# Sums over partitions by transposes, the second half's keys in other PSUM rings, and one 1/rms by way of DRAM, in a hybrid decoder layer

## The chip, the cores and the metric

The kernel runs on one core of a Trainium2 chip. The metric is the device time of one execution in microseconds; lower is better. The core has a matrix engine (TensorE, PE in the profile), VectorE (DVE), ScalarE (ACT), GpSimd (POOL) and SyncE (SP), whose queue issues most DMAs. All matrix results land in PSUM, eight banks of 128 x 512 f32 values.

## The reference

One decoder layer over 2048 tokens of 1024 channels: a norm, one projection into an HGRN2 head group and a sliding-window attention group, an output projection, a gated MLP with a causal convolution, and a final norm. Cut to what matters here:

```python
def rmsnorm(x, w, eps=EPS):
    xf = x.astype(jnp.float32)
    inv = lax.rsqrt(jnp.mean(xf * xf, axis=-1, keepdims=True) + eps)
    return (xf * inv * w.astype(jnp.float32)).astype(x.dtype)

u = rmsnorm(h, norm_mix_w[l])
proj = u @ w_in[l]
...
h = h + mix @ w_out[l]
v = rmsnorm(h, norm_ffn_w[l])
gate = causal_depthwise_conv(v @ w_gate[l], conv_w[l], conv_b[l])
h = h + (jax.nn.silu(gate) * (v @ w_up[l])) @ w_down[l]
...
return rmsnorm(h, final_norm_w)
```

Each of the three norms needs, for each token, the sum of the squares over 1024 channels, and 1/rms from it.

## The kernel before

Activations are kept transposed: channels on the 128 partitions, tokens along the row. The sequence is worked in two halves of 1024 tokens (`hf`, `HALF`), and a half in two token halves `lo` and `hi` of 512. Every matrix product is made of three products of split operands (`hi` and `lo` parts, in fp32r), each a matmul over 512 tokens.

A half goes through these stages: keys and values (`first_unit`, twice: the list `kv`), the heads in an order written out by hand (`ORDER`, with `hgrn` and `attend`), the output projection (`out_proj`), gate and up products (`gate_up`) and the down product (`down`). Gate, up and down use a scheme with seven products instead of eight (`PRODUCTS`: P1, P5, P6, P3, P7, P2, P4, in six pieces each). `down` of the first half also loads and squares the x of the second half, and at its end issues the second half's `kv` and the first `f` product (L1008 to L1010), with the remaining norm work hooked in between their matmuls by `then`. In the last half the product P4 is made token block by token block instead, in `last_rows` (L1013), with tokens on the partitions, and its results leave through the output `rows`.

The program is written out by a tile framework. It places each instruction on its engine in an order that comes from its own model of times, gives tiles their slots, and adds the semaphore waits. On the chip each engine then runs its own queue in that fixed order.

PSUM has three rings: `mm` with four banks, `hg` and `at` with two each; `aux` (L72) names the last two. `unit` (L189) takes one bank for each token half, from `mm`, or from `hg` and `at` for `kind="aux"`. In `down` the products P1, P6, P7 and P4 sit in `mm` (tile `pdx`), P5, P3 and P2 in `hg` and `at` (tile `pdy`).

The norm's 1/rms goes in three steps.

- `Stats.add` (L232) adds squares over the channel blocks into `acc`, 128 partitions by 512 or 1024 tokens.
- `Stats.inverse` (L239) sums over the partitions: for each chunk of 128 tokens one matmul, with the chunk as the stationary operand and a column of ones as the moving one, gives a column with one token per partition (tile `pst`, L245). `rsqrt` (L156) then makes 1/rms on DVE, 13 small instructions on 128 x 4 or 128 x 8 values (L159 to L169).
- `Stats.spread` (L250) brings 1/rms back to all partitions: for each chunk one transpose of the broadcast column (tile `pinv`, L258), and for each 512 tokens a copy by ACT out of PSUM into `acc` (L261).

In `down`, `s1` holds the sums of the final norm for `lo`, `s2` those for `hi`. `finish` (L1081) multiplies the eight blocks of h by 1/rms on DVE (L1084) and sends them out on SP's queue (L1085). For `s2` it runs while P4 is still being made or, in the last half, inside `last_rows`; for `s1` of the first half it runs during the second half's `kv`. `last_rows` makes its own sums of `s1` (L1034) for the partial mean of each token row (`base`), and for each block of 128 tokens takes 1/rms on DVE, scales the rows out of PSUM, and later transposes 1/rms (L1073) for the channels that stay transposed.

Of the kernel before, what the change touches and what calls it, by code (L numbers as in the profile page):

```python
# [8 lines left out]
F32 = mybir.dt.float32  # L9
# [4 lines left out]
ALU = mybir.AluOpType  # L14
AX = mybir.AxisListType
PSUM = bass.MemoryType.PSUM

P = 128
D = 1024
# [7 lines left out]
ATT_J = 4  # L27
# [3 lines left out]
EPS = 1e-6  # L31
# [18 lines left out]
def hymba_layer(ctx: ExitStack, tc: tile.TileContext, a: dict, out: bass.AP, rows_out: bass.AP):  # L50
    nc = tc.nc
# [11 lines left out]
    dp = pool("dram", space=bass.MemoryType.DRAM)  # L63
# [5 lines left out]
    def ps(kind, name):  # L69
        return spaces[kind].tile([P, 512], F32, tag=kind, name=name)  # L70

    aux = ("hg", "at")  # L72

    def halves():
# [5 lines left out]
    ones = cp.tile([P, P], F32, name="ones")  # L80
    nc.vector.memset(ones, 1.0)
    ident = cp.tile([P, P], F32, name="ident")
# [5 lines left out]
                            base=0, pattern=[[-1, P]], channel_multiplier=1)  # L88
# [64 lines left out]

    made = []

    def rsqrt(ss, n, scale, keep=None):  # L156

        ms = sp.tile([P, n], F32, tag=f"ms{n}", name="ms")
        nc.vector.tensor_scalar(ms, ss, scale, EPS, op0=ALU.mult, op1=ALU.add)  # L159
        y = sp.tile([P, n], F32, tag=f"y{n}{keep}", name="y")  # L160
        yi = y.bitcast(I32)
        nc.vector.tensor_scalar(yi, ms.bitcast(I32), 1, None, op0=ALU.logical_shift_right)
        nc.vector.tensor_scalar(yi, yi, -1.0, float(0x5F3759DF), op0=ALU.mult, op1=ALU.add)
        nc.vector.tensor_scalar(ms, ms, -0.5, None, op0=ALU.mult)
        t = sp.tile([P, n], F32, tag=f"t{n}", name="t")
        for _ in range(3):
            nc.vector.tensor_tensor(t, y, y, op=ALU.mult)
            nc.vector.tensor_tensor(t, t, ms, op=ALU.mult)
            made.append(nc.vector.scalar_tensor_tensor(y, t, 1.5, y, op0=ALU.add, op1=ALU.mult))  # L169
        return y  # L170
# [51 lines left out]
    class Stats:  # L222
# [16 lines left out]
        def inverse(self, keep):  # L239

            n = self.acc.shape[-1]
            nt = n // P
            st = ps("hg", "pst")
            for c in range(nt):
                nc.tensor.matmul(st[:, c:c + 1], self.acc[:, c * P:(c + 1) * P], ones[:, 0:1],  # L245
                                 start=True, stop=True)
            self.rs = rsqrt(st[:, 0:nt], nt, 1.0 / D, keep)
            return made[-1]

        def spread(self, bank=None):  # L250

            n = self.acc.shape[-1]
            w = min(n, 512)
            for b in range(n // w):
                pb = ps(aux[b % 2 if bank is None else bank], "pinv")[:, 0:w]
                for c in range(w // P):
                    i = b * w // P + c
                    nc.tensor.transpose(pb[:, c * P:(c + 1) * P], self.rs[:, i:i + 1].to_broadcast([P, P]), ident)  # L258
                if bank is not None:
                    return pb  # L260
                nc.scalar.copy(self.acc[:, b * w:(b + 1) * w], pb)  # L261

    def inv_tile():
        return xp.tile([P, HALF], F32, tag="inv", name="invb", bufs=1)
# [44 lines left out]
            st.add(x)  # L309
        return st  # L310

    def first_unit(X, W, i, then={}):
        return unit(tuple(W[i]) if W else a["w_att"][ATT_J + i], X, "kv", then=then)

    def blocks(t, turn=False):

# [541 lines left out]
    def down(hf, kept, acts, p):  # L858
# [54 lines left out]
        hh = []  # L913
# [37 lines left out]
        for k, (name, _, _, j) in enumerate(todo):  # L951
            if k + 2 < len(todo):
                ready[k + 2] = prep_piece(k + 2)
            if j == 0:
                if name == "P1":
                    bx = o = [ps("mm", "pdx") for _ in range(4)]
                elif name in ("P5", "P2"):
                    by = o = [ps(aux[d % 2], "pdy") for d in range(4)]
                else:
                    o = by if name == "P3" else bx  # L960
                if name == "P3":
                    acc = inv_tile() if final else wp.tile([P, HALF], F32, tag="raw", name="sums", bufs=RAW)
                    s1, s2 = [Stats(acc[:, bs], lambda: p.tile([P, 512], F32, tag="ut", name="fsq", bufs=UT))
                              for bs in (lo, hi)]
                if name == "P2" and not final:
                    stage = iter(("xh2", "xl2") * (KT // 2))
                    loading = load(hf + 1, X, lambda: p.tile([P, HALF], F32, tag=next(stage), name="x", bufs=6))
            if not final and k >= end - 3:
                xs = next(loading, xs)
            if final and k == end:  # L970
                break
            if k == end + 1:
                s2.inverse("o2")
            elif k == end + 3:
                s2.spread()
                finish(hf, hh, s2, hi, nc.sync)
            for d in range(4):
                product(k, o[d], d)
            if j + 1 < NP:
                continue  # L980
            for d in range(4):
                h1, h2 = hh[d], hh[d + 4]
                if name in ("P1", "P2"):
                    add(h1[:, lo], o[d])
                elif name in ("P6", "P3"):
                    add(h1[:, hi], o[d])
                elif name in ("P5", "P7"):
                    add(h2[:, hi], o[d])
                    if final and name == "P7":
                        add(h2[:, lo], o[d])  # L990
                else:
                    add(h2[:, lo], o[d])
                if name == "P3":
                    done(s2, d, hi)
                elif name == "P7":
                    done(s2, d + 4, hi)
                elif name == "P2":
                    done(s1, d, lo)
                elif name == "P4":
                    done(s1, d + 4, lo)  # L1000
        if final:
            for k in range(end + 3, len(todo)):
                ready[k] = prep_piece(k)
            last_rows(hf, hh, s1, fw, ready, range(end, len(todo)), p,
                      {(0, 1): lambda: s2.inverse("o2"),
                       (0, 3): lambda: (s2.spread(), finish(hf, hh, s2, hi, nc.sync))})
            return None
        kv = [first_unit(X, None, 0, {3: lambda: s1.inverse("o"), 7: lambda: xs.inverse("x")})]  # L1008
        kv.append(first_unit(X, None, 1, {2: lambda: (s1.spread(), finish(hf, hh, s1, lo, nc.sync)), 4: xs.spread}))
        f0 = unit(a["w_f"][0], X, "f", kind="aux")  # L1010
        return X, kv, xs.acc, xs.rs, f0

    def last_rows(hf, hh, st, fw, ready, pieces, p, then):  # L1013
# [9 lines left out]
        for tb in range(4):  # L1023
# [5 lines left out]
            for n, k in enumerate(pieces):  # L1029
                then.pop((tb, n), lambda: None)()  # L1030
                if (tb, n) == (0, 4):
                    sb = ps("hg", "pst")
                    for c in range(4):
                        nc.tensor.matmul(sb[:, c:c + 1], st.acc[:, c * P:(c + 1) * P], ones[:, 0:1],  # L1034
                                         start=True, stop=True)
                    base = sp.tile([P, 4], F32, tag="base", name="base")
                    nc.vector.tensor_scalar(base, sb[:, 0:4], 1.0 / D, EPS, op0=ALU.mult, op1=ALU.add)
                    half = sp.tile([P, 4], F32, tag="half", name="half")
                    nc.vector.tensor_scalar(half, base, -0.5, None, op0=ALU.mult)
                if (tb, n) == (0, 5):  # L1040
                    o1 = ps("at", "rows1")
                    for d in range(4):
                        nc.tensor.transpose(o1[:, d * P:(d + 1) * P], hh[d][:, 3 * P:4 * P], ident)
                    y1 = ut("y1")
                    nc.scalar.copy(y1, o1)
                (ah, al), (wh, wl) = ready[k]
                for i in range(wh.shape[1]):
                    l = k == pieces[-1] and i + 1 == wh.shape[1]
                    nc.tensor.matmul(o, ah[:, i, ts], wh[:, i], start=False, stop=False, skip_group_check=True)
                    nc.tensor.matmul(o, ah[:, i, ts], wl[:, i], start=False, stop=False, skip_group_check=True)  # L1050
                    nc.tensor.matmul(o, al[:, i, ts], wh[:, i], start=False, stop=l, skip_group_check=True)
# [29 lines left out]
    def finish(hf, hh, st, bs, eng, inv=None):  # L1081
        for d in range(KT):
            t = hh[d][:, bs]
            nc.vector.tensor_tensor(t, t, st.acc if inv is None else inv, op=ALU.mult)  # L1084
            eng.dma_start(out[d, :, hf * HALF + bs.start:hf * HALF + bs.stop], t)  # L1085

    X, W = [], []
# [105 lines left out]
```

## Time and profile before

| what | us |
|---|---|
| median of 3 runs | 2155.03 |
| lowest and highest | 2154.21, 2155.93 |
| profiled execution, device time | 2156.06 |
| profiled execution, span from first to last instruction | 2154.3 |
| mean granted TensorE clock in it | 0.999 |

The profile is one execution. Its span starts with the first instruction and ends with the last; the device time has a little more around it. In a timeline row stand the start in us from the span's beginning, the duration in us, the engine, the source line, the operation, the output tile and the input tiles, the shapes and the count of merged instructions; a bracket tells how long the engine was idle before and what released it. PEld is the loading of TensorE's stationary operand. Of a matmul's inputs the moving one is named first. Busy time of matmuls overlaps, so what a matmul costs is read from the starts of the ones around it.

### The profile page before, as it was taken

Reading aid. Unit: us, or ns where it says so; the run is one execution under the profiler, and the core shown is the slowest. Engines: PE = TensorE matmul, PEld = TensorE weight load, DVE = VectorE, ACT = ScalarE, POOL = GpSimd, SP = SyncE. Lnnn points to the kernel's source line nnn. Section 1 sums busy time; section 2 is a strip of 40 time slices with the busy share of each in tenths; the row PEclk is TensorE's granted clock in tenths of the full one; section 3 lists DMA queues with packets and bytes.
Section 4 is the critical chain, followed back from the end, with each engine's and each line's share of the span. In section 5 each row is a group of like instructions: output and inputs, shape, how many; then the busy total and the mean of one; then the engine's idle time right before and its main releaser. Section 6 shows DMA issues by size and latency. Waiting matters only on the chain.

```text
span 2154.3 us, 29259 instructions
## 1 busy us (share of the span) xinstructions
PE 2136.6 (99%) x11319; PEld 1797.8 (83%) x11319; DVE 1622.7 (75%) x2431; ACT 1021.1 (47%) x1818; POOL 19.5 (1%) x45
## 2 busy tenths in 40 slices
PE   8999999999999999999999999999999999999998
PEld 7988988888888888888889889888888888888887
DVE  6576767788887878785865767677888788787865
ACT  5445553564444445335634446525544444443453
POOL 2000000000000000000000000000000000000000
PEclk9999999999999999999999999999999999999999
DMA  4111112423232334964641101124233323259743
GB/s 158 40 30 40 31 30 79 137 70 126 83 127 84 113 107 158 382 231 161 201 137 33 37 30 31 40 74 157 70 105 101 119 84 127 88 190 395 236 147 132
DMA packets 91148, 254.42 MB, mean 118 GB/s; under 512 B 11137, under 2 KB 13953, under 8 KB 91009
## 3 DMA queue, kind: packets, MB, share of 16 engines
q1 hardware_dynamic: 90576, 252.29, 35.0%
q8 instruction: 89, 1.46, 0.3%
q14 instruction: 51, 0.41, 0.1%
q10 hardware_dynamic: 432, 0.27, 0.0%
HBM read 195.37 MB, written 57.15 MB: 117 GB/s over the span
## 4 chain that ended last, share of the span: by engine, by line
PE 94%; DVE 3%; ACT 1%; DMA 1%; issue 1%; SPq 0%; DVEq 0%; ACTq 0%
PE X L753 7%; PE X L755 7%; PE X L754 7%; PE pop L204 7%; PE f L204 4%; PE q L204 4%; PE hq L204 4%; PE Y L754 4%; PE Y L753 4%; PE Y L755 4%; PE g L204 3%; PE pdy L940 3%; PE pdx L940 3%; PE pdx L941 3%; PE pdx L942 3%; PE pdy L941 3%
## 5 line engine op out<-in xcount | busy, mean ns | idle before, releaser
L628 ACT CAST whi<-raw 128x1024 fp32r<-128x1024 f32 x88 | 92.5, 1051 | 101.7 <-PE X L754 68.3
L824 DVE SCALAR_TENSOR_TENSOR y<-ga,cw,y 128x1024 f32<-128x1024 f32 x88 | 112.2, 1277 | 37.7 <-ACT y L822 37.7
L753 PE MATMUL X<-T,whi 128*128 128x512 f32 x352 | 136.9, 389 | 0.0
L754 PE MATMUL X<-T,whi 128*128 128x512 f32 x352 | 136.9, 389 | 0.0
L755 PE MATMUL X<-T,wlo 128*128 128x512 f32 x352 | 136.9, 389 | 0.0
L629 DVE TENSOR_TENSOR wlo<-raw,whi 128x1024 fp32r<-128x1024 f32 x88 | 107.1, 1217 | 5.6 <-ACT whi L628 5.6
L185 ACT CAST whi<-raw 128x1024 fp32r<-128x1024 f32 x58 | 60.5, 1048 | 103.1 <-issue 20.6
L759 ACT COPY u<-X 128x512 f32<-128x512 f32 x88 | 51.7, 588 | 99.6 <-PE X L755 99.4
L629 DVE TENSOR_TENSOR xld<-raw,xhd 128x1024 fp32r<-128x1024 f32 x72 | 80.8, 1130 | 10.4 <-ACT xhd L628 10.3
L628 ACT CAST xhd<-raw 128x1024 fp32r<-128x1024 f32 x72 | 69.4, 977 | 35.9 <-DMA raw<-act0B 10.7
L204 PE MATMUL pop<-XL,whi 128*128 128x512 f32 x256 | 84.2, 392 | 0.9 <-DVE XL L216 0.9
L204 PE MATMUL pop<-XH,wlo 128*128 128x512 f32 x256 | 83.3, 391 | 0.8 <-DVE wlo L186 0.8
L204 PE MATMUL pop<-XH,whi 128*128 128x512 f32 x256 | 83.2, 396 | 0.8 <-ACT XH L215 0.5
L186 DVE TENSOR_TENSOR wlo<-raw,whi 128x1024 fp32r<-128x1024 f32 x58 | 70.3, 1216 | 11.0 <-ACT whi L185 11.0
L753 PEld LDWEIGHTS X<-T,whi 128*128 128x128 f32 x352 | 66.1, 188 | 13.7
L755 PEld LDWEIGHTS X<-T,wlo 128*128 128x128 f32 x352 | 66.1, 188 | 13.7
L754 PEld LDWEIGHTS X<-T,whi 128*128 128x128 f32 x352 | 66.1, 188 | 13.7
L759 ACT COPY s<-X 128x512 f32<-128x512 f32 x44 | 25.9, 588 | 106.4 <-PE X L755 106.4
L621 PE MATMUL pvv<-whi,XL 128*128 128x256 f32 x256 | 73.0, 286 | 0.0
L620 PE MATMUL pvv<-whi,XH 128*128 128x256 f32 x256 | 72.9, 286 | 0.0
L622 PE MATMUL pvv<-wlo,XH 128*128 128x256 f32 x256 | 72.1, 285 | 0.0
L753 PE MATMUL X<-T,Sh 128*128 128x512 f32 x176 | 68.7, 390 | 0.0
(390 smaller groups left out, 6440.2 us busy)
## 6 DMA issues: line engine op xcount, KB each, us to landing
wr<-in_w_down SPq DMA_DIRECT2D x90, 512.0 KB, 5.7
raw<-in_w_gate SPq DMA_DIRECT2D x44, 512.0 KB, 3.6
raw<-in_w_up SPq DMA_DIRECT2D x44, 512.0 KB, 3.6
raw<-act0T SPq DMA_DIRECT2D x20, 512.0 KB, 5.4
raw<-act1T SPq DMA_DIRECT2D x20, 512.0 KB, 5.0
act0B<-y SPq DMA_DIRECT2D x33, 256.0 KB, 2.6
act1B<-y SPq DMA_DIRECT2D x33, 256.0 KB, 2.3
raw<-in_w_out SPq DMA_DIRECT2D x16, 512.0 KB, 3.7
```

Of the source, the lines that this page charges most:

```text
L204: nc.tensor.matmul(o[b], w, x[:, bs], start=f, stop=l)
L620: nc.tensor.matmul(o[:, 0:256], xh[:, t], hi[:, c], start=kt == 0, stop=False)
L621: nc.tensor.matmul(o[:, 0:256], xl[:, t], hi[:, c], start=False, stop=False)
L628: nc.scalar.copy(h, src)
L629: return (eng or nc.vector).tensor_tensor(l, src, h.bitcast(F32), op=ALU.subtract)
L753: nc.tensor.matmul(o, wh[:, ws], xh, start=i == 0 and not more, stop=False, skip_group_check=more)
L754: nc.tensor.matmul(o, wh[:, ws], xl, start=False, stop=False, skip_group_check=more)
L755: nc.tensor.matmul(o, wl[:, ws], xh, start=False, stop=i == 3, skip_group_check=more)
L759: nc.scalar.copy(t, o)
L824: nc.vector.scalar_tensor_tensor(y, g[:, w:w + HALF], C.cw[:, ft, w:w + 1], y, op0=ALU.mult, op1=ALU.add)
L940: nc.tensor.matmul(o, wh[:, i, c], ah[:, i, cols], start=f, stop=False, skip_group_check=more)
L941: nc.tensor.matmul(o, wh[:, i, c], al[:, i, cols], start=False, stop=False, skip_group_check=more)
```

## The change

There are three edits.

1. Sums over partitions: a new helper `sums` transposes up to four chunks of `acc` into one bank and lets DVE add each transposed chunk along the row. `rsqrt` calls it where `keep` is given, which is in every `Stats.inverse`; eight chunks take one bank of `hg` and one of `at`. `last_rows` calls it for `base`. The heads' own norm (`rsqrt(ss, TT, 1.0 / P)`) is as before.
2. Keys of the second half: the first of the two `kv` units takes its banks from `hg` and `at`, and the `f` product behind them from `mm`. In the first half `kv` and `f` are as before.
3. 1/rms of `s2` in both halves: `spread_far` writes the 128 x 4 values as one row of 512 into DRAM and loads that row to all 128 partitions, both by DMAs of GpSimd's queue, in place of the transposes and the copy of `spread`.

```diff
+    def sums(dst, acc):
+
+        n = acc.shape[-1] // P
+        for c0 in range(0, n, 4):
+            k = min(4, n - c0)
+            st = ps(aux[c0 // 4 % 2], "pst")
+            for c in range(k):
+                nc.tensor.transpose(st[:, c * P:(c + 1) * P], acc[:, (c0 + c) * P:(c0 + c + 1) * P], ident)
+            nc.vector.tensor_reduce(dst[:, c0:c0 + k], st[:, 0:k * P].rearrange("p (c t) -> p c t", c=k),
+                                    axis=AX.X, op=ALU.add)
+
     def rsqrt(ss, n, scale, keep=None):
 
         ms = sp.tile([P, n], F32, tag=f"ms{n}", name="ms")
+        if keep:
+            sums(ms, ss)
+            ss = ms
         nc.vector.tensor_scalar(ms, ss, scale, EPS, op0=ALU.mult, op1=ALU.add)
...
-            st = ps("hg", "pst")
-            for c in range(nt):
-                nc.tensor.matmul(st[:, c:c + 1], self.acc[:, c * P:(c + 1) * P], ones[:, 0:1],
-                                 start=True, stop=True)
-            self.rs = rsqrt(st[:, 0:nt], nt, 1.0 / D, keep)
+            self.rs = rsqrt(self.acc, nt, 1.0 / D, keep)
             return made[-1]
...
+    def spread_far(st, dst):
+
+        row = dp.tile([1, 512], F32, name="row")
+        nc.gpsimd.dma_start(row.rearrange("o (c p) -> (o p) c", p=P), st.rs)
+        nc.gpsimd.dma_start(dst, row.to_broadcast([P, 512]))
...
-    def first_unit(X, W, i, then={}):
-        return unit(tuple(W[i]) if W else a["w_att"][ATT_J + i], X, "kv", then=then)
+    def first_unit(X, W, i, then={}, kind="mm"):
+        return unit(tuple(W[i]) if W else a["w_att"][ATT_J + i], X, "kv", kind=kind, then=then)
...
             elif k == end + 3:
-                s2.spread()
+                spread_far(s2, s2.acc)
                 finish(hf, hh, s2, hi, nc.sync)
...
-                       (0, 3): lambda: (s2.spread(), finish(hf, hh, s2, hi, nc.sync))})
+                       (0, 3): lambda: (spread_far(s2, s2.acc), finish(hf, hh, s2, hi, nc.sync))})
...
-        kv = [first_unit(X, None, 0, {3: lambda: s1.inverse("o"), 7: lambda: xs.inverse("x")})]
+        kv = [first_unit(X, None, 0, {3: lambda: s1.inverse("o"), 7: lambda: xs.inverse("x")}, "aux")]
         kv.append(first_unit(X, None, 1, {2: lambda: (s1.spread(), finish(hf, hh, s1, lo, nc.sync)), 4: xs.spread}))
-        f0 = unit(a["w_f"][0], X, "f", kind="aux")
+        f0 = unit(a["w_f"][0], X, "f")
...
-                    sb = ps("hg", "pst")
-                    for c in range(4):
-                        nc.tensor.matmul(sb[:, c:c + 1], st.acc[:, c * P:(c + 1) * P], ones[:, 0:1],
-                                         start=True, stop=True)
                     base = sp.tile([P, 4], F32, tag="base", name="base")
-                    nc.vector.tensor_scalar(base, sb[:, 0:4], 1.0 / D, EPS, op0=ALU.mult, op1=ALU.add)
+                    sums(base, st.acc)
+                    nc.vector.tensor_scalar(base, base, 1.0 / D, EPS, op0=ALU.mult, op1=ALU.add)
```

## The prediction

> **What bounds the kernel now.** I read the totals and the chain of the page first, then the engine waits, and then TensorE's (PE's) timeline at each place that the diff touches.
>
> ```profile
> span 2154.3 us, 29259 instructions
> PE 2136.6 (99%) x11319; PEld 1797.8 (83%) x11319; DVE 1622.7 (75%) x2431; ACT 1021.1 (47%) x1818; POOL 19.5 (1%) x45
> ...
> PE 94%; DVE 3%; ACT 1%; DMA 1%; issue 1%; SPq 0%; DVEq 0%; ACTq 0%
> ...
> PE kv L204 <- ACT XH L218: 5.9, 1, 5.9
> ```
>
> The first two lines are the span and the busy times, the third is the chain that ended last by engine, the last is the longest wait of PE (total, times, longest). PE is nearly the whole chain, and what it waits longest for is one wait of 5.9 us, for the first input. So an edit is worth what it takes out of PE's instruction stream, or puts between two of its matmuls. Work of DVE (VectorE), ACT and the queues counts only when PE, or the last rows behind PE, waits for it.
>
> **The sums over partitions.** Before, four 128x1 matmuls make the sums of 512 tokens; the trace has each of them as two passes. After, four transposes do it, and DVE adds up along the row.
>
> ```profile
> L245 PE MATMUL pst<-ones,invb 128*128 128x1 f32 x72 | 8.4, 242 | 0.0
> L258 PE MATMUL pinv<-ident,y 128*128 128x128 f32 x44 | 5.9, 272 | 0.0
> ...
> L245 PE MATMUL pst<-ones,sums 128*128 128x1 f32 x16 | 1.9, 239 | 0.0
> L1034 PE MATMUL pst<-ones,invb 128*128 128x1 f32 x8 | 0.9, 240 | 0.0
> ```
>
> 72 + 16 + 8 = 96 passes are 48 chunks of 128 tokens, or 12 groups of four. The mean of one matmul (242, 272 ns) misleads, because matmuls overlap; the starts tell the cost:
>
> ```profile
> 1047.91 0.39 PE L942 MATMUL pdx<-xh2d,lod 128*128 128x512 f32 x1
> 1048.14 0.95 PE L245 MATMUL pst<-ones,sums 128*128 128x1 f32 x8
> ...
> 1049.74 0.40 PE L940 MATMUL pdx<-xh2d,gad 128*128 128x512 f32 x1
> ...
> 1078.16 0.39 PE L204 MATMUL kv<-XL,whi 128*128 128x512 f32 x1
> 1078.38 0.60 PE L258 MATMUL pinv<-ident,y 128*128 128x128 f32 x4
> ...
> 1079.52 0.39 PE L204 MATMUL kv<-XH,whi 128*128 128x512 f32 x1
> ```
>
> Full-width matmuls start 0.227 us apart (1047.91 to 1048.14). In both extracts the last row is the fourth full-width matmul after the first, so 0.91 us would lie between them without the group. There are 1.83 us with the sums and 1.36 with four transposes: **0.92 us against 0.45**. The transposes here have the shape of the new ones (128 columns of the identity, a 128x128 stationary block in f32). Twelve groups save 12 x 0.47 = **5.6 us**.
>
> DVE gets 12 reductions of 128x512 out of PSUM; the trace has none.
>
> ```profile
> L428 DVE TENSOR_TENSOR po<-ppt,ownT 128x512 f32<-128x512 f32 x32 | 21.8, 683 | 1.9 <-PE ppt L425 1.9
> L401 DVE TENSOR_REDUCE m<-sc 128x8 f32<-128x1024 f32 x16 | 19.4, 1214 | 0.2
> ```
>
> A 512-column read of PSUM takes 0.68 us, a reduction of twice the elements 1.21, hence 0.61: between 0.6 and 0.7 us each, some 8 us on an engine that is idle for a quarter of the span. I cost it at nothing, because the chain from the sums to the transposes of 1/rms ends early on DVE:
>
> ```profile
> 463.24 0.16 DVE L169 SCALAR_TENSOR_TENSOR y<-t,y 128x8 f32<-128x8 f32 x1
> ...
> 467.43 1.01 PEld L258 LDWEIGHTS pinv<-ident,y 128*128 128x128 f32 x8
> ...
> 1091.40 0.17 DVE L169 SCALAR_TENSOR_TENSOR y<-t,y 128x8 f32<-128x8 f32 x1
> ...
> 1096.82 1.03 PE L258 MATMUL pinv<-ident,y 128*128 128x128 f32 x8
> ```
>
> From the last step of 1/rms to its transposes there are 4.0 us in the gated MLP and 5.3 at the change of halves; one or two reductions take at most 1.4 of that. Were this cover gone, each of the seven places with sums would cost PE up to 1.4 us. The sums of eight chunks also take a bank of the second auxiliary ring, `at`; it is free again after the reduction, before the products `Y` and `Z` and the transposes at 467 us ask for the rings.
>
> **1/rms of the last norm's second token half by DRAM.** On PE, `s2.spread()` goes twice, each one group of four transposes: 2 x 0.45 = **0.9 us**. Two ACT copies go too, worth nothing on an engine busy 47%. Added are two DMAs on the queue of POOL (GpSimd), the second waiting for the first: 512 single numbers to a row in DRAM, then the row to all partitions. Behind them in POOL's queue stand only memsets of `ST` for the heads to come (POOL is busy 19.5 us in all). Eight DVE multiplications wait for the second DMA, and behind these, in DVE's order, stand the sums of the first token half and of the next half's x; on SP eight output DMAs wait, with weight loads behind them.
>
> ```profile
> 1074.85 0.15 DVE L169 SCALAR_TENSOR_TENSOR y<-t,y 128x4 f32<-128x4 f32 x1
> ...
> 1080.55 4.91 DVE L1084 TENSOR_TENSOR h<-h,sums 128x512 f32<-128x512 f32 x8 [0.27 <-ACT sums L261]
> ...
> 2123.04 0.16 DVE L169 SCALAR_TENSOR_TENSOR y<-t,y 128x4 f32<-128x4 f32 x1
> 2127.59 4.91 DVE L1084 TENSOR_TENSOR h<-h,invb 128x512 f32<-128x512 f32 x8 [4.39 <-ACT invb L261]
> ...
> 2138.82 0.38 PE L1073 MATMUL pinv<-ident,yr 128*128 128x128 f32 x2
> ...
> fw<-in_final_norm_row SPq DMA_DIRECT2D x1, 256.0 KB, 3.1
> rows<-y ACTq DMA_DIRECT2D x2, 128.0 KB, 2.2
> nmw<-in_norm_mix_w ACTq DMA_DIRECT2D x1, 4.0 KB, 3.2
> battn<-in_b_attn SPq DMA_DIRECT2D x1, 3.0 KB, 8.6
> ```
>
> Before, the multiplications start 5.5 and 4.4 us after 1/rms is done. No DMA of POOL is in the trace; the last column of the DMA rows is the time from issue to landing. A broadcast of a row like the second DMA took 3.1 us, a small load of 32-byte pieces 3.2; the lower bound is two of the fastest, 4.4, the upper two of the slowest, 17.2. I take 3.2 + 3.1 = 6.3, the nearest rows, a little later than now by 0.8 and 1.9 us, and cost it at nothing: the first case has the 5.3 us of the next 1/rms in front of PE, and in the second PE has the transposes of the last rows (`yr`) only at 2138.82, where the DVE work in between ends 4.4 us earlier:
>
> ```profile
> 2134.11 0.33 DVE L1061 TENSOR_SCALAR yr<-tr,yr 128x1 f32<-128x1 f32 x2
> ```
>
> The Trainium skill, page "DMA: Bandwidth & Descriptors", section "Anatomy of one DMA — SWDGE (gpsimd) path", gives about 2.0 us fixed plus bytes by 436 GB/s for a DMA of this queue; an estimate by it is 2.0 and 2.6 us for the two, and the sum would stay as it is.
>
> **The second half's keys in the other rings.** `kv[0]` no longer takes its banks in `mm`, which hold the last product `P4`, but in `hg` and `at`, whose last product, `P2`, is read out while PE is at `P4`.
>
> ```profile
> 1073.34 0.39 PE L942 MATMUL pdx<-xh2d,lod 128*128 128x512 f32 x1
> 1074.41 0.47 PE L204 MATMUL kv<-XH,whi 128*128 128x512 f32 x1 [0.68 <-DVE t L168]
> ```
>
> The step over the joint is 1.07 us instead of 0.227: **0.84 us** saved, since what ends PE's wait is DVE, which at that moment turns to the additions that empty the `mm` banks. What is late next: `kv[1]` and `f0` take the four `mm` banks about 11 us later, long after DVE has read them. Until keys and values are scaled, `hg` and `at` have one bank left each, so the sums of s1 and of x, and the two spreads, take turns in it; the 5.3 us of slack above pay for that.
>
> **The clock.** Behind two neighbouring groups of sums the granted clock dips, and PE slows down to half:
>
> ```profile
> 1083.61 0.94 PE L245 MATMUL pst<-ones,sums 128*128 128x1 f32 x8
> ...
> 1085.45 1.84 PE L245 MATMUL pst<-ones,invb 128*128 128x1 f32 x16
> ...
> 1086.00:1088.00 2.00, 2.00 (x15) 1.92 (x15) 1.62 (x15) 0.00 (x0) 0.00 (x0) 0.92 0.83 301
> 1088.00:1090.00 2.00, 2.00 (x6) 1.52 (x6) 1.09 (x8) 1.04 (x1) 0.00 (x0) 0.50 0.05 19
> 1090.00:1092.00 2.00, 2.00 (x8) 1.57 (x7) 1.50 (x4) 0.00 (x0) 0.00 (x0) 0.73 0.00 0
> ```
>
> In the stretches the third figure from the right is the clock: 2 x (0.08 + 0.50 + 0.27) = **1.7 us** lost. The 24 passes take 0.9 + 1.8 us of some 3.7. After, 12 transposes stand there, 1.3 us (twelve of 0.11). I count the dip as gone; should it stay, the sum is 1.7 us smaller.
>
> **Sum.** 5.6 + 0.9 + 0.84 + 1.7 = 9.0 us. The profiled execution took 2156.06 us, 1.8 around its span, so **2147.0 us**. The median of the runs is 2155.03, their ends 2154.21 and 2155.93: 1.7 apart, one dip. The lowest, taken as one without it, less the other 7.3, gives 2146.9, the same.
>
> **Rivals.**
> 1. DVE or POOL is a few us late and PE pays part of it. For it: all three edits lengthen the path to 1/rms around 1075 to 1097 us, and two banks take turns. Against: 4.0 to 5.3 us of slack at each place. Seven places at up to 1.4 us are 9.8; a fifth to three fifths of that gives 2149 to 2153.
> 2. Slower: the round trip through DRAM holds up DVE's queue. With R the time from 1/rms to the landing, DVE starts R - 5.5 and R - 4.4 us later, of which 5.3 and 4.4 are slack (the rows above); PE loses 2R - 19.6, once R is over some 10 us. At the upper bound R = 17.2 that is 14.8 us: 2161.8. It turns the gain into a loss from R = 14 on. For it: a DMA of 3 KB took 8.6 us, and 512 separate 4-byte writes are in no row. Against: the 8.6 was at the start, behind other loads.
> 3. Transposes let the clock fall. If they count as idle, a dip could follow each of the seven places with sums: seven dips of 1.7 are 11.9, which makes 2147.0 + 11.9 = 2158.9, the present dip among them. Against it stand 16 transposes among small matmuls, at a clock of 1.00:
>
> ```profile
> 359.18 1.09 PE L425 MATMUL ppt<-ident,sc 128*128 128x128 f32 x8
> ...
> 360.74 1.06 PE L554 MATMUL pkn<-ident,K 128*128 128x128 f32 x8
> ...
> 360.00:362.00 2.00, 1.80 (x13) 1.16 (x11) 2.00 (x4) 0.65 (x3) 0.00 (x0) 1.00 0.00 0
> ```
>
> The Trainium skill, page "TensorE: Matmul & The Clock Gate", section "Part 4: PE-mode transpose", says that a transpose does not count as PE-busy in the same way. By that rule this rival would be likely; these rows disagree with it, and so I leave it little.
> 4. The order of the whole program changes with the edits, for the scheduler places instructions by its own times. PE's small waits may shrink or grow; I allow 2 us either way, the ends of my forecast.
>
> **How the numbers follow.** Forecast 0.73 (2144.5 to 2149), rival 1 0.15, rival 2 0.07, rival 3 0.05; rival 4 is the forecast's width. The range, 2144.5 to 2153.0, takes in the forecast and rival 1. A measurement tells about 0.2%, 4.3 us, from no change: faster means under 2150.7. That is the forecast and some of rival 1, 0.79; the same the rest of rival 1 and half of rival 3, 0.12; slower 0.09.
>
> **What would show it.** Right: groups of `pst` by four transposes that cost 0.45 us; no step over 0.3 us at the joint; a clock of 1.00 from the joint to 1100 us; no `pinv` transposes for s2; reductions of 0.6 to 0.7 us. Wrong: a PE wait at `pst`, `pinv` or `yr`; an idle time of several us before DVE's eight multiplications, with the sums behind them late; new steps at half clock after the transposes.

## The result and the profile after

| kernel | median, us | lowest and highest | ratio to before, 95% interval | span of the profiled execution |
|---|---|---|---|---|
| before, measured beside it | 2155.48 (4 runs) | 2154.21, 2157.22 | | 2154.3 |
| after | 2166.41 (4 runs) | 2165.55, 2167.34 | 1.0051, 1.0039 to 1.0063 | 2165.6 |

The changed kernel is half a per cent slower. The forecast was 2147.0, and the range ended at 2153.0, so both missed; the sign was wrong too. The profiled execution of after took 2167.34, with a mean granted clock of 0.995 in place of 0.999.

The page of after: its span, its busy times and the chain that ended last, by engine.

```profile
span 2165.6 us, 29217 instructions
PE 2135.2 (99%) x11263; PEld 1794.6 (83%) x11263; DVE 1632.2 (75%) x2443; ACT 1018.9 (47%) x1816; POOL 24.4 (1%) x49
...
PE 58%; issue 36%; DVE 3%; DMA 2%; ACT 1%; POOL 0%; SPq 0%; POOLq 0%; DVEq 0%; ACTq 0%
```

PE's busy time fell by only 1.4 us (2136.6 to 2135.2), while the span grew by 11.3. So PE stands idle some 13 us longer. Its work must also have become slower somewhere, because the change took instructions worth several us out of its stream. PE fell from 94% of the chain to 58%, but the 36% of "issue" is no loss of that size. It is nearly all one piece of the chain:

```profile
303.62 775.88 issue
1079.51 8.99 DMA row<-y
```

The chain went through the new DMA `row<-y` and from there back along POOL's queue, which had been idle for 775.88 us ahead of that DMA. So the row tells which transfer the chain ran through, and not that PE was idle. PE's waits, in total, times and longest, are the first place to look for what was lost:

```profile
PE pst L163 <- DVE ms L164: 7.1, 1, 7.1
PE pinv L1086 <- DVE yr L1074: 6.4, 1, 6.4
PE kv L218 <- ACT XH L232: 5.9, 1, 5.9
...
PE X L771 <- DVE wlo L645: 0.8, 2, 0.4
```

The third row is the wait for the first input, the same as before. The first two are new, 13.5 us together: one for a PSUM bank that a reduction (`ms`) has to release, at the change of halves, and one for `yr` in the last rows. Both name DVE. DVE's own timeline shows why it was late; the bracket is its idle time and what ended it:

```profile
1079.05 0.15 DVE L183 SCALAR_TENSOR_TENSOR y<-t,y 128x4 f32<-128x4 f32 x1
...
1093.61 4.90 DVE L1097 TENSOR_TENSOR h<-h,sums 128x512 f32<-128x512 f32 x8 [12.55 <-DMA sums<-row]
1098.44 1.28 DVE L164 TENSOR_REDUCE ms<-pst 128x4 f32<-128x512 f32 x2
...
2127.87 0.16 DVE L183 SCALAR_TENSOR_TENSOR y<-t,y 128x4 f32<-128x4 f32 x1
...
2142.98 4.90 DVE L1097 TENSOR_TENSOR h<-h,invb 128x512 f32<-128x512 f32 x8 [9.77 <-DMA invb<-row]
2147.80 0.20 DVE L1068 TENSOR_SCALAR msr<-ssr,base 128x1 f32<-128x1 f32 x1
```

The first and the fourth of these rows are the last steps of the two 1/rms of `s2`. From there to the multiplications there are 1093.61 - 1079.20 = 14.4 us and 2142.98 - 2128.03 = 14.95 us; before, 5.5 and 4.4. In this time DVE is idle for 12.55 and 9.77 us, although nothing but the eight multiplications needs the row. What stands behind them in DVE's queue is, in the first half, the reduction that releases the bank PE waits for, and, in the last half, the 1/rms of the second block of rows. The multiplications then take 4.9 us more, and only after them does PE go on (the bracket again):

```profile
1099.17 1.12 PE L163 MATMUL pst<-ident,invb 128*128 128x128 f32 x4 [7.09 <-DVE ms L164]
...
2149.70 0.45 PE L1086 MATMUL pinv<-ident,yr 128*128 128x128 f32 x1 [6.37 <-DVE yr L1074]
```

The four transposes of the first row take 1.12 us; where the clock is full the same four took 0.60. The stretches tell the rest. Of the three figures at the end of a row the first is the granted clock, and the first pair behind the length of the stretch is PE's busy time:

```profile
1094.00:1098.00 4.00, 0.00 (x0) 0.00 (x0) 4.00 (x8) 0.00 (x0) 0.00 (x0) 0.51 0.73 268
1098.00:1102.00 4.00, 2.83 (x9) 2.44 (x10) 3.83 (x12) 0.00 (x0) 0.00 (x0) 0.50 0.86 269
1102.00:1106.00 4.00, 4.00 (x14) 3.15 (x14) 3.45 (x20) 1.05 (x1) 0.00 (x0) 0.71 0.31 118
...
2148.00:2152.00 4.00, 2.31 (x6) 1.93 (x7) 3.71 (x19) 0.98 (x4) 0.00 (x0) 0.50 0.86 294
2152.00:2156.00 4.00, 4.00 (x11) 3.09 (x10) 1.11 (x4) 0.00 (x0) 0.00 (x0) 0.55 0.52 162
```

The clock halves while PE waits and stays halved for 5 to 6 us after PE is back at work. An estimate of what that costs is PE's busy time in each stretch, times the share of the clock that is missing: 2.83 x 0.50 + 4.00 x 0.29 = 2.6 us behind the first wait and 2.31 x 0.50 + 4.00 x 0.45 = 3.0 behind the second.

**Where the time went.** Losses: 7.1 + 6.4 of waits and 2.6 + 3.0 of half clock, 19.1 us. The span grew by 11.3. What is left over, 7.8 us, is what the change must have saved, against 9.0 of the forecast.

What the new path itself takes is in the timeline of POOL, which issues both DMAs, and in the table of DMAs (the last figure is the time from issue to landing):

```profile
1079.51 0.92 POOL L276 DMA_DIRECT2D row<-y  x1 [775.89 <-DVE y L183]
...
1088.80 0.55 POOL L277 DMA_DIRECT2D sums<-row  x1 [7.82 <-DMA row<-y]
```

```profile
sums<-row POOLq DMA_DIRECT2D x1, 256.0 KB, 4.8
...
row<-y POOLq DMA_DIRECT2D x2, 2.0 KB, 8.9
```

The small transfer is the slow one: 2 KB in 512 pieces of 4 bytes took 8.9 us, 256 KB in rows of 2 KB took 4.8. The prediction had 3.2 and 3.1. For most of the 8.9 us no DMA engine is at work. In these stretches the last two figures are the mean busy share of the DMA engines and what they moved in GB/s:

```profile
1081.00:1081.50 0.50, 0.50 (x3) 0.40 (x3) 0.06 (x1) 0.00 (x0) 0.00 (x0) 1.00 0.40 4
1081.50:1086.00 4.50, 4.50 (x25) 3.83 (x24) 0.00 (x0) 1.05 (x1) 0.00 (x0) 1.00 0.00 0
```

Two us after the issue the engines fall idle, and the landing comes some 7 us later. What happens in between the trace does not show.

### The profile page after: what moved, and what is told of

Read it like the earlier page. It is cut to its first block, busy times and chain, and to the rows that moved or that the text cites. A ratio compares the mean times of both kernels' runs of the same rounds, so it can differ in the third digit from the quotient of the medians.

```text
span 2165.6 us, 29217 instructions
## 1 busy us (share of the span) xinstructions
PE 2135.2 (99%) x11263; PEld 1794.6 (83%) x11263; DVE 1632.2 (75%) x2443; ACT 1018.9 (47%) x1816; POOL 24.4 (1%) x49
## 4 chain that ended last, share of the span: by engine, by line
PE 58%; issue 36%; DVE 3%; DMA 2%; ACT 1%; POOL 0%; SPq 0%; POOLq 0%; DVEq 0%; ACTq 0%
PE q L218 4%; PE hq L218 4%; PE f L218 4%; PE X L771 4%; PE X L770 4%; PE X L769 4%; PE pop L218 3%; PE g L218 2%; PE Y L769 2%; PE Y L770 2%; PE Y L771 2%; PE pvv L637 1%; PE pvv L636 1%; PE pvv L638 1%; PE pdx L958 1%
## 5 line engine op out<-in xcount | busy, mean ns | idle before, releaser
L771 PE MATMUL X<-B,wlo 128*128 128x512 f32 x176 | 68.7, 390 | 0.8 <-DVE wlo L645 0.8
```

Of the source, the lines that this page charges most:

```text
L771: nc.tensor.matmul(o, wl[:, ws], xh, start=False, stop=i == 3, skip_group_check=more)
```

## The experiments

The kernel before, run beside each group on the same chip, had medians of 2154.68, 2154.49 and 2154.54; each ratio is to the one beside it. The question was first which edit brings the loss, then whether it is the length of the trip through DRAM or the place of the multiplications in DVE's queue, and what makes the trip long.

**One: each edit by itself.** `sums_only` is edit 1 alone: the changed kernel with `spread` back in both places and the rings as before.

```diff
-                spread_far(s2, s2.acc)
+                s2.spread()
...
-                       (0, 3): lambda: (spread_far(s2, s2.acc), finish(hf, hh, s2, hi, nc.sync))})
+                       (0, 3): lambda: (s2.spread(), finish(hf, hh, s2, hi, nc.sync))})
...
-        kv = [first_unit(X, None, 0, {3: lambda: s1.inverse("o"), 7: lambda: xs.inverse("x")}, "aux")]
+        kv = [first_unit(X, None, 0, {3: lambda: s1.inverse("o"), 7: lambda: xs.inverse("x")})]
...
-        f0 = unit(a["w_f"][0], X, "f")
+        f0 = unit(a["w_f"][0], X, "f", kind="aux")
```

> Edit 1 alone (sums by transposes; keys in mm and s2's spread on TensorE as before). Theory (the DRAM round trip is what costs): no wait of TensorE over 1 us beyond those of before, 12 groups at 0.45 instead of 0.92 us, so 5.6 us less than before, and up to 1.7 more if the half-clock window at the change of halves goes: 2148 to 2150 us. Rival (transposes and reductions themselves cost: late 1/rms or half-clock windows after them): at or above before, 2155 or more, with waits at pinv or clock dips behind pst.

Measured: 2150.86, ratio 0.9981 (0.9972 to 0.9990), which is 0.9 above the expected range. `sums_rings` has edits 1 and 2, that is, only the first two replacements above.

> Edits 1 and 2 (the changed kernel with s2's spread on TensorE as before). Theory: the wait of 7 us at pst goes, because DVE no longer stands behind the DMA; 2147 to 2149 us, 0.8 less than edit 1 alone. Rival (the rings: keys hold one bank of hg and at, and the sums take turns in the other): TensorE still waits several us at pst, 2152 us or more.

Measured: 2150.44, ratio 0.9978 (0.9970 to 0.9987), and 2150.18 in a later group; expected were 2147 to 2149. Edit 1 is a gain of 3.8 us, less than the 5.6 of its sums alone. The step over the joint is gone with edit 2, but the medians are only 0.4 apart and their intervals overlap: what edit 2 is worth by itself was not told from nothing. PE's timeline of `sums_only` at the joint shows why so little was left for it:

```profile
1072.72 0.39 PE L958 MATMUL pdx<-xh2d,lod 128*128 128x512 f32 x1
1073.04 0.66 PE L163 MATMUL pst<-ident,invb 128*128 128x128 f32 x4
1073.81 0.47 PE L218 MATMUL kv<-XH,whi 128*128 128x512 f32 x1
```

With edit 1 a group of four transposes already stands in the gap. Of the 1.09 us from 1072.72 to 1073.81, 0.45 are the group and 0.23 the usual step, so 0.41 us were left to save, not 0.84.

`dram_only` is edit 3 alone, put on the kernel before (with the helper `spread_far` added).

```diff
-                s2.spread()
+                spread_far(s2, s2.acc)
...
-                       (0, 3): lambda: (s2.spread(), finish(hf, hh, s2, hi, nc.sync))})
+                       (0, 3): lambda: (spread_far(s2, s2.acc), finish(hf, hh, s2, hi, nc.sync))})
```

> Edit 3 alone (s2's 1/rms by DRAM in both halves, all else as before). Theory: DVE stands idle for 10 us or so before the eight multiplications in both halves, TensorE waits behind it in the last rows (6 us and a half-clock window of 3) and less at the change of halves, where both banks of hg are free; 2160 to 2170 us. Rival (the loss needs the rings): only the last rows lose, and the first half shows no wait of TensorE over 1 us; 2158 to 2164.

Measured: 2170.76, ratio 1.0073 (1.0060 to 1.0085), 0.8 above the expected range. Edit 3 alone loses 16.1 us, without transposed sums and without the other rings. PE's waits in it:

```profile
PE pinv L1079 <- DVE yr L1067: 5.8, 1, 5.8
...
PE pinv L258 <- DVE t L167: 5.3, 1, 5.3
```

At the change of halves PE now waits at the transposes of the next 1/rms, not at a ring's bank. So where PE meets the late DVE depends on the rest of the program; in both of these programs it meets it in both places.

**Two: the two places apart.** `dram_first` is the changed kernel with `spread` back in the last half only, `dram_last` with `spread` back in the first half only (the two replacements of the first diff, one each).

> The changed kernel with the DRAM trip in the first half alone (the last half spreads s2 on TensorE as before). Theory: only the wait at pst (7 us) and its half-clock window remain, 9 to 10 us above edits 1 and 2 alone: 2158 to 2161 us. Rival (the two places aren't independent): above 2162 or below 2156.

> The changed kernel with the DRAM trip in the last half alone. Theory: only the wait at yr (6.4 us) and its half-clock window (2.8) remain, 8 to 9 us above edits 1 and 2 alone: 2157 to 2160 us; and the losses of the two single trips add up to that of both (16 us). Rival (not independent): above 2161 or below 2155.

Measured: 2157.48, ratio 1.0012 (1.0003 to 1.0021), and 2158.38, ratio 1.0016 (1.0007 to 1.0024). Against `sums_rings` that is 7.0 for the first half, with a wait of 5.8 at `pst`, and 7.9 for the last, with a wait of 6.3 at `yr`. The first is half a us below the range that was expected, the second inside its range. Each costs more than its wait. By the estimate of above, the half clock behind the waits costs 2.0 and 2.5 us here, and the spread that is saved gives 0.45 back: 5.8 + 2.0 - 0.45 = 7.35 and 6.3 + 2.5 - 0.45 = 8.35, within half a us of what was measured. The two add up to 15 of the 16.0 us between `sums_rings` and after (2166.41).

**Three: the place in DVE's queue.** If the loss comes from what stands behind the waiting multiplications, it must vanish when they stand further back, with the trip as long as it is. `late_finish` issues them later in the program's text.

```diff
                 spread_far(s2, s2.acc)
-                finish(hf, hh, s2, hi, nc.sync)
...
-                       (0, 3): lambda: (spread_far(s2, s2.acc), finish(hf, hh, s2, hi, nc.sync))})
+                       (0, 3): lambda: spread_far(s2, s2.acc),
+                       (2, 4): lambda: finish(hf, hh, s2, hi, nc.sync)})
...
+                                              6: lambda: finish(hf, hh, s2, hi, nc.sync)}))
```

> The changed kernel with the eight multiplications of s2 issued later (behind s1's in the second kv unit; in the last rows in the third block), the two DMAs where they are. Theory (it is DVE's queue, not the DMA as such): the DMAs take 14 us as before, and both waits of TensorE go; 2145 to 2149 us. Rival (the DMAs themselves disturb, or POOL's queue does): the waits stay, 2160 or more.

Measured: 2165.41, ratio 1.0048 (1.0034 to 1.0062), a miss. It says nothing against the theory, because the edit did not do what it was to do. DVE's timeline in it:

```profile
1092.23 4.90 DVE L1098 TENSOR_TENSOR h<-h,sums 128x512 f32<-128x512 f32 x8 [12.54 <-DMA sums<-row]
```

The multiplications stand where they stood, with the same idle time before them (12.54 us against 12.55), so writing them later did not move them in the queue. `ordered_finish` therefore ties them down: in the first half they are placed behind the last step of the 1/rms of x, in the last half behind the 1/rms of the third block of rows.

```diff
+            self.last = made[-1]
...
+    def after(ins, work):
+        with tc.issue_after(ins.ins):
+            work()
...
-                finish(hf, hh, s2, hi, nc.sync)
...
+                       (0, 3): lambda: spread_far(s2, s2.acc),
+                       (3, 0): lambda: after(marks["row"], lambda: finish(hf, hh, s2, hi, nc.sync))})
...
+                                              6: lambda: after(xs.last, lambda: finish(hf, hh, s2, hi, nc.sync))}))
...
+                marks["row"] = nc.vector.tensor_scalar(y, t, 1.5, y, op0=ALU.add, op1=ALU.mult)
```

> The changed kernel, with the eight multiplications of s2 forced on DVE's queue behind the 1/rms of the next half's x (first half) and behind the third block's 1/rms (last half); the two DMAs stay where they are. Theory (DVE's queue carries the round trip to TensorE): the round trip stays at 14 to 15 us, no wait of TensorE over 1 us at pst, pinv or yr, no half-clock window before the end, 2148.5 to 2150.5 us, as edits 1 and 2 alone or 0.9 less. Rival (the DMAs, POOL's queue or the DRAM row disturb by themselves): 2160 us or more.

Measured: 2148.76, ratio 0.9971 (0.9960 to 0.9981): 17.65 us below after, which was measured in another group. The DMA table and DVE's timeline of it:

```profile
row<-y POOLq DMA_DIRECT2D x2, 2.0 KB, 10.5
```

```profile
1095.27 9.72 DVE L1103 TENSOR_TENSOR h<-h,sums 128x512 f32<-128x512 f32 x16 [3.53 <-DMA sums<-row]
```

This is the run that decides. The trip is no shorter (10.5 us to landing, against 8.9), and DVE still waits 3.53 us for it, yet neither `pst` nor `yr` is among PE's waits and the clock does not fall: nothing that PE needs stands behind the waiting instruction any more. The queue carries the loss, and the length of the trip only sets its size.

**Four: why the trip is long.** Either a DMA of this queue is slow here, or 512 pieces of 4 bytes are. `sync_queue` sends both DMAs by SP.

```diff
-        nc.gpsimd.dma_start(row.rearrange("o (c p) -> (o p) c", p=P), st.rs)
-        nc.gpsimd.dma_start(dst, row.to_broadcast([P, 512]))
+        nc.sync.dma_start(row.rearrange("o (c p) -> (o p) c", p=P), st.rs)
+        nc.sync.dma_start(dst, row.to_broadcast([P, 512]))
```

> The changed kernel with both DMAs of the DRAM trip on SP's queue instead of POOL's. Theory a (the 512 pieces of 4 bytes are slow on any queue): the first DMA still takes 8 us or more, both waits of TensorE stay, 2162 to 2167 us. Theory b (POOL's queue is slow): the first DMA lands in 2 to 4 us, the trip takes 6 to 8 instead of 14 to 15, the waits of TensorE shrink below 2 us, 2148 to 2153 us.

Measured: 2166.51, ratio 1.0054 (1.0040 to 1.0068), as slow as after, with waits of 6.8 and 6.3. The DMA table:

```profile
row<-y SPq DMA_DIRECT2D x2, 2.0 KB, 9.5
```

`wide_pieces` keeps POOL's queue and changes the order of the row, so that each partition's four values lie side by side: 128 pieces of 16 bytes. The multiplications then read 1/rms with a stride.

```diff
-        nc.gpsimd.dma_start(row.rearrange("o (c p) -> (o p) c", p=P), st.rs)
+        nc.gpsimd.dma_start(row.rearrange("o (p c) -> (o p) c", p=P), st.rs)
...
+            if bs.start:
+                v = t.rearrange("p (c q) -> p c q", q=P)
+                nc.vector.tensor_tensor(v, v, st.acc.rearrange("p (q c) -> p c q", q=P), op=ALU.mult)
```

> The changed kernel with the DRAM row in another order, so that the first DMA writes 128 pieces of 16 bytes instead of 512 of 4, and the eight multiplications read it with a stride. Theory a (the time goes with the number of pieces): the first DMA lands in 3 to 5 us instead of 9, the trip takes 9 to 10, the waits of TensorE shrink from 7 and 6 to some 2 us each and bring no half-clock window: 2149 to 2156 us. Theory b (a fixed time of a write to DRAM): it stays at 8 us or more, 2163 us or more.

Measured: 2151.40, ratio 0.9985 (0.9976 to 0.9993). The DMA table, the groups of instructions (one half's multiplications: busy time and mean ns of one, then the idle time before them), and PE's waits:

```profile
row<-y POOLq DMA_DIRECT2D x2, 2.0 KB, 2.1
```

```profile
L1099 DVE TENSOR_TENSOR h<-h,invb 128x512 f32<-128x512 f32 x8 | 8.0, 1071 | 1.3 <-DMA invb<-row 1.3
```

```profile
PE pst L163 <- DVE ms L164: 1.3, 1, 1.3
...
PE pinv L1086 <- DVE yr L1074: 0.9, 1, 0.9
```

The same 2 KB land in 2.1 us instead of 8.9; 3 to 5 were expected. PE's waits shrink to 1.3 and 0.9 us, and behind these two the clock does not fall. The pieces are what makes the trip long, the queue that issues it is not. Their number and their size changed together, so these runs do not tell which of the two it is.

**Five: both cures, and the best version.** `wide_ordered` is `ordered_finish` with the row of `wide_pieces`; `ordered_2` and `sums_rings_2` repeat `ordered_finish` and `sums_rings` side by side.

> ordered_finish with the wide pieces. Theory: the trip was hidden there already, so a shorter one changes nothing: 2148 to 2150 us, within 1 us of ordered_finish. Rival (the trip still costs there): 1 us or more below it.

> ordered_finish once more, beside edits 1 and 2 alone: if the two groups of transposes that the DRAM trip takes off TensorE are worth their 0.9 us once the trip is hidden, 0.5 to 2 us below sums_rings_2; if the trip brings no gain at all, the same.

> Edits 1 and 2 alone once more, beside ordered_finish on the same chip: 2150 to 2151 us.

Measured: 2151.06, ratio 0.9984 (0.9975 to 0.9993); 2148.47, ratio 0.9973 (0.9963 to 0.9984); 2150.18, ratio 0.9979 (0.9970 to 0.9988). The shorter trip makes the ordered kernel slower by 2.6 us, a miss. DVE's timelines near the end, first of `ordered_2`, then of `wide_ordered`:

```profile
2134.45 2.50 DVE L1103 TENSOR_TENSOR h<-h,invb 128x512 f32<-128x512 f32 x4
...
2142.45 0.88 DVE L1083 SCALAR_TENSOR_TENSOR sqr<-rows,yr,fw 128x256 f32<-128x256 f32 x2
```

```profile
2134.37 4.00 DVE L1105 TENSOR_TENSOR h<-h,invb 128x512 f32<-128x512 f32 x4
...
2145.01 0.88 DVE L1083 SCALAR_TENSOR_TENSOR sqr<-rows,yr,fw 128x256 f32<-128x256 f32 x2
```

Four multiplications take 4.00 us instead of 2.50, and twice four stand ahead of the last rows, whose scaling comes 2.56 us later. That is the whole difference. With nothing waiting behind the trip, its length is worth nothing, and the strided reading is paid at the end of the kernel. `ordered_2` is the fastest version, 6.1 us below before; with `spread` in place of the trip (`sums_rings_2`) it is 1.7 us slower. The intervals of the two ratios overlap, but the runs themselves do not: the seven of `ordered_2` lie between 2147.93 and 2149.58, the eleven of `sums_rings_2` between 2149.69 and 2150.94. The two also differ in where the eight multiplications stand, so the 1.7 us are not the hidden trip's alone.

## Why the prediction was wrong, point by point

**The step that failed** is the cost of the trip through DRAM: "I take 3.2 + 3.1 = 6.3, the nearest rows, a little later than now by 0.8 and 1.9 us, and cost it at nothing". The trip measured 14.4 and 14.95 us, up to the multiplications that wait for it. The prediction had written down that 512 separate 4-byte writes are in no row, and still took for them the row of a small load in 32-byte pieces; `wide_pieces` shows that the pieces make the difference, 8.9 us against 2.1. Its upper bound of 17.2 did hold the trip, but the range of the time did not reach to the case that goes with it, because that case had only 0.07. Even that case, 2161.8, lies below the 2166.41 that was measured. The estimate by the Trainium skill, page "DMA: Bandwidth & Descriptors", section "Anatomy of one DMA — SWDGE (gpsimd) path", 2.0 us for the first DMA, was off in the same direction, and so no check on the row. It is a fixed time and a time by bytes, with no term for pieces: the 16-byte pieces agree with it (2.1 us) and the 4-byte pieces do not (8.9).

**Rival 2 is what happened, at a higher price.** Its mechanism, its two places and its queue are those of the trace, and `ordered_finish` shows that the queue is the cause. With the measured trips its formula gives (14.4 - 10.8) + (14.95 - 8.8) = 9.8 us, hence 2156.8. Two things were missing from it:

- The slack in the first half. The formula counted 5.3 us there, taken from before's transposes of the next 1/rms. In `dram_only` this holds: its multiplications start 16.3 us after 1/rms (1091.55 - 1075.21 in the rows below), the formula gives 5.5, and PE waits 5.3. With edits 1 and 2 PE meets DVE earlier, at a bank of the small ring that only a reduction on DVE releases, and waits 7.1 instead of 3.6. The prediction saw that banks would take turns there and let the same 5.3 us pay for it. In the last half the formula gives 6.15, and 6.4 was measured. DVE's timeline of `dram_only`:

```profile
1075.06 0.15 DVE L169 SCALAR_TENSOR_TENSOR y<-t,y 128x4 f32<-128x4 f32 x1
...
1091.55 4.90 DVE L1090 TENSOR_TENSOR h<-h,sums 128x512 f32<-128x512 f32 x8 [11.40 <-DMA sums<-row]
```

- The clock. The prediction had a clock term for the sums' small matmuls, none for PE standing idle. The half clock behind the two waits is 5.6 us by the estimate of above. It belonged in rival 2's price, and makes a shorter trip than R = 14 turn the gain into a loss. The Trainium skill, page "TensorE: Matmul & The Clock Gate", section "Why this matters for your kernels", warns of idle gaps of TensorE over about 3 us between matmuls, after which the clock falls to half. The traces agree as far as they go, with falls behind waits of 7.1 and 6.4 us (5.3 in `dram_only`) and none behind 1.3 and 0.9. They have no wait in between, and in after the clock fell 2.0 and 2.1 us after the end of PE's last matmul.

With these the sum is 2147.0 + 13.5 of waits + 5.6 of half clock + 1.2 of savings that did not come = 2167.3, the profiled execution. The 1.2 is the remainder (9.0 less 7.8), so the sum closes by itself; where the 1.2 went is looked for below.

**The other terms: the prices held, their sum did not quite.** PE's timeline of after shows a group of four transposes among full-width matmuls, and the joint:

```profile
1047.03 0.39 PE L958 MATMUL pdx<-xh2d,lod 128*128 128x512 f32 x1
1047.26 0.60 PE L163 MATMUL pst<-ident,sums 128*128 128x128 f32 x4
1047.62 0.48 PE L956 MATMUL pdx<-xh2d,gad 128*128 128x512 f32 x1
1047.94 0.39 PE L957 MATMUL pdx<-xl2d,gad 128*128 128x512 f32 x1
...
1071.99 0.39 PE L958 MATMUL pdx<-xh2d,lod 128*128 128x512 f32 x1
1072.21 0.62 PE L218 MATMUL kv<-XH,whi 128*128 128x512 f32 x2
```

From 1047.03 to 1047.94 there are 0.91 us, of which 0.45 are two full-width steps: 0.46 for the group, 0.45 forecast. The step over the joint (1071.99 to 1072.21) is 0.22 us, where it was 1.07. A reduction takes 0.68 us (680 ns in the mean of eleven), forecast 0.6 to 0.7. The spread of s2 and the old dip in the clock are gone.

What was lost is one new step in each gated MLP, where PE waits for DVE (`X` for `wlo`, two times, in the first extract of waits). `sums_only` has the same waits and so they belong to edit 1. PE's timeline of `sums_rings` shows one of them:

```profile
453.64 0.40 PE L771 MATMUL X<-T,Sl 128*128 128x512 f32 x1
454.41 0.51 PE L771 MATMUL X<-B,wlo 128*128 128x512 f32 x1 [0.37 <-DVE wlo L645]
454.76 0.40 PE L769 MATMUL X<-B,whi 128*128 128x512 f32 x1
```

The two steps are 0.77 and 0.35 us instead of 0.23 each, so one such place costs 0.66 us, more than the wait alone, and the two cost 1.3: about as much as the 1.2 that did not come in after. This is rival 1 in small: PE comes to `wlo` earlier than before, and DVE does not (it starts this `wlo` at 453.14 us, before at 453.06).

By themselves, edits 1 and 2 gave 4.2 us against the before beside them. Against the 2156.06 from which the prediction subtracts they gave 5.6 (to 2150.44), in place of 5.6 + 0.84 + 1.7 = 8.1. Of the 2.5 that are missing, 1.3 are the two steps above. Another 0.8 stands at the very start of the profiled execution, in front of everything the edits touch: full-width matmuls start 0.43 us apart there until 10.5 us, until 9 in before. The last 0.4 us were not traced.

**Rival 3** is refuted: behind groups of transposes alone, as in `sums_rings`, no half-clock stretch appears before PE has made its last matmul. **The sign**: "faster" got 0.79 because the trip was thought short. Without edit 3, or with it and the queue in order, the kernel is faster, by 4.2 to 6.1 us, less than the forecast of 8.0 below the median.

## What to carry to other kernels

An instruction that waits for a DMA can cost what stands behind it in its engine's queue: here it cost 16 us, and nothing once that work stood ahead of it. So before pricing the wait, list what stands behind it. Then either move the waiting instruction back, by a forced order, since later text alone did not move it, or leave the data on chip. Look at the pieces of a DMA before its bytes (2 KB took 8.9 us in pieces of 4 bytes, 2.1 in pieces of 16); when no row of the trace has pieces that small, let the range reach the upper bound. A wait of TensorE of 6 to 7 us cost its length and, by the estimate, 2 to 3 us more of half clock behind it.

## What the runs showed of the hardware that was not expected

- 2 KB from 128 partitions to DRAM took 8.9 us in 512 pieces of 4 bytes (10.5 in `ordered_finish`, 9.5 by SP's queue) and 2.1 us in 128 pieces of 16. At the first of the two places in after the DMA engines were idle from 2.0 to 6.5 us behind the issue, so most of the 6.8 us of difference is no work of theirs that the trace shows.
- Eight products of 128x512 in f32 on DVE take 8.0 us instead of 4.9, that is 1.00 us instead of 0.61 for each, when one operand is read with a stride of 16 bytes.
- The clock fell to half 2.0 and 2.1 us after the end of PE's last matmul in after, 2.9 in `dram_first` and 4.4 in `dram_last`, and came back 4.0 to 5.9 us after PE was at work again. The stretch at half clock lasted 10.2 us in both places of after and 6.8 in `dram_first` and `dram_last`, three times and twice the 3.4 of the dip in before.
